# Part of an output projection's sums made between the HGRN and attention chains of a hybrid decoder layer

## The chip, the cores and the metric

One core of one Trainium2 chip. The metric is the device time of one launch in microseconds (us), the median of several runs. Kernel and reference work in float32.

## The reference

One layer with d = 1024 features and 1024 tokens. What bears on this change is its first third:

```python
x = rmsnorm(h) @ w_in                      # columns for three groups of heads
y = concat(hgrn2_mix(...),                 # 4 heads, 512 columns
           dilated_window_mix(...),        # attention, 4 heads, 256 columns
           rwkv7_mix(...))                 # 4 heads, 256 columns
h = h + y @ w_out                          # the output projection
h = h + conv_glu_ffn(rmsnorm(h), ...)      # d_ff = 2816
h = h + sigmoid(rmsnorm(h) @ w_g) * (p @ w_p)
```

## The kernel before

Activations are held transposed, as 8 row blocks of 128 features by 1024 tokens; a "half" is 512 of the tokens, and a "row half" (m, hf) is row block m of the result for half hf. Weights come as one block `[128, 1024]` (512 KB) per row block of the result: 8 tiles of 128x128, one for each row block k of the input.

**One product.** float32 is split into two fp32r parts, hi and lo, and a product is three matmuls (`mm3`, L132 to L141): hi by hi, lo of the data by hi of the weights, hi of the data by lo of the weights. A row half over all 8 k is thus 24 matmuls of 128x512. Weights are loaded by `load_w` (L102, one DMA on SP's queue into `wraw`, two buffers) and split by `split2` (L110): ScalarE (ACT) casts `whi` at L114, and VectorE (DVE) or GpSimd (POOL), by turns, subtracts `wlo` at L116. Data are split by `split_x` (cast `xh` on ACT at L160, `xl` on DVE or POOL at L162).

**Stages.** `phase_mix` (L321) normalises x and projects it; runs the RWKV heads in two passes (`rwkv`, L461), into which projections are filled as `project_rest` (L392; `FILL`, L494, says how often, and the list `js` in `rwkv` says which); then runs, with each other, four HGRN heads (`hgrn_head`, L836: chain A makes heads 0 and 2, chain B heads 1 and 3), attention (`swa`, L992, chain C) and the projections that are left (`project_late`, L429, chain F, one half of a projection, 24 matmuls into PSUM tile `zp`, per turn). The order of their turns is the string that L338 to L341 build. An input projection's result goes to DRAM as `z` and comes back as `zl` when its head begins (`zload`, L453). When a group of heads is done, its output is split into `O[k]` (`o_split`, L1100): k = 6, 7 are RWKV, k = 0 to 3 the HGRN heads, k = 4, 5 attention. `O` lies in the buffers of the projections' input, so it begins after the last turn of `project_late`.

**Output projection.** `phase_out` (L1107) loads x into `h[k]` by 8 DMAs on ACT's queue (L1114), and for each turn of the list `turns` runs `rows`: the matmuls into a PSUM tile `dp` (pool `dps`, two buffers), the weights of the turn after next, and for each half the addition to `h` on DVE (L1131) and a store of `h` for later (L1132). The turns are row 0 and row 1 with both halves, rows 2 to 7 with half 0, rows 2 to 7 with half 1. The k come in the order 6, 7, 0, 1, 4, 2, 3, 5, so that what is ready first is used first. The sum of squares of half 0 follows row by row, its reciprocal root after row 7, and `ps_ss` (L196) spreads that to all partitions.

**Behind it** comes the FFN. `ffn_first` (L1234) loads the first blocks of its weights (`raw`, L1210, SP's queue) and DVE makes sums of them (L1307, L1309, L1310), which the FFN's products need only later. A scheduler puts the instructions of each engine in order; each engine then runs its own list in order, and a DMA is issued in its turn of the list of the queue that it is on.

Of the kernel before, what the change touches and what calls it, by code (L numbers as in the profile page):

```python
# [10 lines left out]
F32 = mybir.dt.float32  # L11
# [3 lines left out]
ALU = mybir.AluOpType  # L15
# [3 lines left out]
P = 128  # L19
T = 1024  # L20
HT = 512
ND = 8
# [43 lines left out]
def interleave(order, streams):  # L66

    live = dict(streams)
    while live:
        for s in order:  # L70
            if s in live and next(live[s], STOP) is STOP:
                del live[s]


def handover(a, b, steps=14):

    for _ in range(steps):
        next(a)
        yield
    for i, _ in enumerate(b):  # L80
        if i == 1:
            for _ in a:
                yield
        yield
# [5 lines left out]
class Trunk:  # L90
# [230 lines left out]
    def phase_mix(self):  # L321
        nc, tc = self.nc, self.tc
        self.mix_norm()
        with tc.tile_pool(name="slots", bufs=1) as slots:
            self.slots, self.NSLOT = slots, 8
            self.rwkv()
        self.O, self.done = None, []
        for p in (0, 1):
            self.o_split(6 + p)
        with tc.tile_pool(name="hg", bufs=1) as slots, tc.tile_pool(name="sw", bufs=1) as sp:  # L330
            self.slots, self.NSLOT = slots, 11
            self.hgrn_setup()
            self.sp = sp
            self.swmask = sp.tile([P, T], F32, name="swmask")
            nc.scalar.dma_start(self.swmask, self.a["swm"])
            A = handover(self.hgrn_head(0), self.hgrn_head(2))
            B = handover(self.hgrn_head(1), self.hgrn_head(3))
            order = ["C", "A"] + ["M"] * 24  # L338
            for r in range(36):
                order += "C" * (r in self.TURNS) + "A" + "B" * (r > 5) + "F" * (r % 2 and r < 16)  # L340
            interleave(order, {"A": A, "B": B, "C": self.swa(sp), "F": self.project_late(self.rest), "M": self.more})  # L341

    TURNS = [i * 33 // 22 for i in range(1, 23)]

# [84 lines left out]
    def project_late(self, js):  # L429
# [20 lines left out]
        for k in self.done:  # L450
            self.o_split(k)

    def zload(self, j, pool_slot, eng=None):  # L453
        t = pool_slot("zl")
        (eng or self.nc.sync).dma_start(t, self.z[j])
        return t
# [12 lines left out]
    def rwkv(self):  # L469
        nc, tc = self.nc, self.tc  # L470
        lt = self.mix_in(0, 6, "lora")
        nc.scalar.activation(lt[0:64, :], lt[0:64, :], AF.Tanh)
        sg = self.mix_in(1, 7, "sg")
        nc.scalar.activation(sg, sg, AF.Sigmoid)
        self.z = {}
        js = iter((*range(8, 16), 24, 25, 26, 16, 17, 20, 21, 19, 23, 27, 28, 29, 18, 22))
        for p in (0, 1):
            d = {}
            with tc.tile_pool(name=f"pre{p}", bufs=1) as tp:
                self.rwkv_prep(p, tp, lt, d)  # L480
                self.rwkv_inverse(p, tp, d)
            lead, n = self.FILL[p]
            fill = self.project_rest([next(js) for _ in range(n)])
            for _ in range(8 * lead):
                next(fill)
            with tc.tile_pool(name=f"rk{p}", bufs=1) as rp:
                self.rwkv_main(p, rp, sg, d, fill)
            self.rwkv_norm(p, sg, d, 1, fill, 6 - 3 * p)
            if p == 0:
                for _ in fill:  # L490
                    pass
        self.rest, self.more = list(js), fill

    FILL = (5, 10), (4, 9)  # L494

    def rwkv_prep(self, p, tp, lt, d):

# [609 lines left out]
    def phase_out(self, hp, x0, emb):  # L1107


        nc = self.nc  # L1110
        self.h = [hp.tile([P, T], F32, name=f"h{k}") for k in range(ND)]
        self.hd = [[self.zpool.tile([P, HT], F32, tag=f"hd{k}_{hf}", name=f"hd{k}_{hf}") for hf in (0, 1)] for k in range(ND)]
        for k in range(ND):
            nc.scalar.dma_start(self.h[k], self.a["xT"][k])  # L1114
        acc = hp.tile([P, HT], F32, name="acc")

        turns = [(0, (0, 1)), (1, (0, 1)), *((m, (0,)) for m in range(2, ND)), *((m, (1,)) for m in range(2, ND))]
        ws = [self.load_w(self.a["w_out"][m]) for m, _ in turns[:2]]

        def rows(m, halves):  # L1120
            ps = self.dps.tile([P, T], F32, tag="dp", name=self.nm("dp"))
            self.dense([ps[:, :HT], ps[:, HT:]], ws.pop(0), self.O, (6, 7, 0, 1, 4, 2, 3, 5), halves)
            turns.pop(0)
            order = ExitStack()
            if len(turns) > 1:
                ws.append(self.load_w(self.a["w_out"][turns[1][0]]))
                order.enter_context(self.tc.issue_after(self.cast))
            with order:
                for g in halves:
                    u = self.h[m][:, g * HT:(g + 1) * HT]  # L1130
                    nc.vector.tensor_tensor(u, u, ps[:, g * HT:(g + 1) * HT], ALU.add)  # L1131
                    nc.scalar.dma_start(self.hd[m][g], u)  # L1132

        for m in range(ND):
            rows(m, (0, 1) if m < 2 else (0,))
            self.sq_acc(acc, self.h[m][:, :HT], m == 0)
        rows(2, (1,))
        pb = self.rstd_bcast(acc, 1.0 / 1024, EPS, self.mxp)
        x0.close()
        self.TX = {}  # L1140
        for i, n in enumerate(("p1", "p2")):
            self.TX[n] = [[self.tile16(8 * i + 2 * k + c, F32R) for c in (0, 1)] for k in range(4)]
        self.ped = [self.zpool.tile([P, T], F32, tag=f"pe{m}", name=f"pe{m}") for m in range(ND)]
        pwp = emb.enter_context(self.pool("pw"))
        px, pw = [], []
        parts = [(px, self.pxp, "pT", 0), (pw, pwp, "ple_proj", 0), (px, self.pxp, "pT", 1), (pw, pwp, "ple_proj", 1)]
        norm = self.ffn_norm(0, pb)
        for m in range(3, ND):
            rows(m, (1,))
            for _ in range(2):  # L1150
                next(norm, None)
            if parts:
                self.pe_load(pwp, *parts.pop(0))
        for m in range(ND):
            self.sq_acc(acc, self.h[m][:, HT:], m == 0)
        pb = self.rstd_bcast(acc, 1.0 / 1024, EPS, self.mxp)
        self.ffn_first()
        for m in range(5):
            self.embed(m, pw, px, self.dps.tile([P, T], F32, tag="dp", name=self.nm("dp")))
        self.pe_in = (pw, px)  # L1160
        return pb
# [552 lines left out]
```

## Time and profile before

| | |
|---|---|
| median of 3 runs | 1476.78 us (1476.26 to 1476.89) |
| time of the profiled execution | 1476.02 us |
| its span | 1474.2 us |
| TensorE's granted clock, mean | 0.992 |
| PE busy | 1420.9 us (96%) |
| DVE / ACT / POOL busy | 1053.9 / 595.8 / 383.1 us |
| RWKV with its filler | about 120 to 436 us of the span |
| HGRN and attention with `project_late` | 437 to 625 us |
| output projection | 625 to 682 us |

Times within the span are in us from its start. "busy" of an engine is time in which it executes; the rest it waits. PE is TensorE's matmul side, and its clock is the share of full speed that the chip granted. In a timeline row the columns are start, duration, engine, line, operation, output and inputs, tile sizes, and in brackets the idle time just before it and what ended it. A row of a table by stretches gives, behind each stretch, its length and the busy us (with the instructions started) of PE, PEld, DVE, ACT and POOL, then TensorE's clock, the busy share of the DMA engines and GB/s.

### The profile page before, as it was taken

To read this page: it belongs to the slowest core of one execution; us is meant where nothing else is said; L and a number is where in the kernel's file an instruction comes from. 1 tells how busy PE (TensorE), PEld (TensorE's weight loads), DVE (VectorE), ACT (ScalarE), POOL (GpSimd) and SP (SyncE) were. 2 spreads that over 40 slices of the span, in tenths; PEclk is the share of its full clock that TensorE was granted. 3 is DMA by queue.
4 is the path that set the end of the run, shared out by engine and by line. 5 is a ranking of instruction groups with operands and counts; after the bars stand their busy time and mean duration, and the time that the engine had idled before them with its cause. 6 is when DMAs were issued, how large, how long until landed. Compare 5 with 4: busy or idle time off the path is not lost.

```text
span 1474.2 us, 23335 instructions
## 1 busy us (share of the span) xinstructions
PE 1420.9 (96%) x9198; PEld 1153.4 (78%) x9198; DVE 1053.9 (71%) x1559; ACT 595.8 (40%) x984; POOL 383.1 (26%) x280
## 2 busy tenths in 40 slices
PE   6999999999999988899999999999999999999996
PEld 4778878787787666788778888888888888888885
DVE  6486243782465688647879888888888799767775
ACT  6512211313124455425544444444434544455552
POOL 2221011210122322222044444445544000002432
PEclk9999999999999999999999999999999999999998
DMA  5124102132061121174323333332333883351352
GB/s 213 43 79 133 41 31 89 47 108 80 31 228 58 58 77 54 44 279 161 135 83 114 108 102 105 108 106 96 105 108 103 312 292 97 105 163 58 119 173 101
DMA packets 79533, 167.67 MB, mean 114 GB/s; under 512 B 19904, under 2 KB 22208, under 8 KB 79424
## 3 DMA queue, kind: packets, MB, share of 16 engines
q1 hardware_dynamic: 66032, 146.39, 29.8%
q10 hardware_dynamic: 12368, 15.99, 3.1%
q0 software_dynamic: 1024, 3.80, 0.7%
q8 instruction: 72, 1.18, 0.3%
q14 instruction: 37, 0.30, 0.1%
HBM read 119.76 MB, written 46.40 MB: 113 GB/s over the span
## 4 chain that ended last, share of the span: by engine, by line
PE 48%; issue 2%; DVE 2%; POOL 1%; DMA 0%; ACT 0%; POOLq 0%; DVEq 0%; ACTq 0%
PE bg L1201 15%; PE bv L1201 12%; PE bv L1495 7%; PE bg L1495 7%; PE bv L137 1%; PE bv L139 1%; PE bv L141 1%; PE bg L137 1%; PE bg L139 1%; PE bg L141 1%; PE dp L137 1%; PE dp L139 1%; PE dp L141 1%; POOL wlo L116 0%; DVE h L1227 0%
## 5 line engine op out<-in xcount | busy, mean ns | idle before, releaser
L137 PE MATMUL dp<-xh,whi 128*128 128x512 f32 x560 | 193.0, 405 | 10.5 <-ACT xh L377 9.9
L139 PE MATMUL dp<-xl,whi 128*128 128x512 f32 x560 | 187.2, 394 | 1.2 <-DVE xl L378 1.1
L141 PE MATMUL dp<-xh,wlo 128*128 128x512 f32 x560 | 186.5, 393 | 0.3 <-POOL wlo L116 0.3
L116 POOL TENSOR_TENSOR wlo<-wraw,whi 128x512 fp32r<-128x512 f32 x60 | 82.0, 1367 | 325.5 <-ACT whi L114 290.4
L116 POOL TENSOR_TENSOR wlo<-raw,whi 128x512 fp32r<-128x512 f32 x84 | 134.8, 1624 | 76.1 <-ACT whi L114 76.1
L114 ACT CAST whi<-wraw 128x512 fp32r<-128x512 f32 x120 | 73.0, 617 | 171.9 <-PE dp L139 131.2
L1201 PE MATMUL bg<-t,whi 128*128 128x512 f32 x352 | 133.2, 389 | 0.0
L137 PEld LDWEIGHTS dp<-xh,whi 128*128 128x128 f32 x560 | 102.1, 188 | 36.2 <-ACT xh L377 9.9
L139 PEld LDWEIGHTS dp<-xl,whi 128*128 128x128 f32 x560 | 104.7, 188 | 26.0 <-DVE xl L378 3.1
L141 PEld LDWEIGHTS dp<-xh,wlo 128*128 128x128 f32 x560 | 105.3, 188 | 23.9 <-issue 1.0
L116 POOL TENSOR_TENSOR wlo<-s,whi 128x512 fp32r<-128x512 f32 x44 | 64.2, 1459 | 171.7 <-ACT whi L114 158.0
L1495 PE MATMUL bg<-t,whi 128*128 128x512 f32 x308 | 95.2, 390 | 0.0
L1495 PE MATMUL bv<-t,whi 128*128 128x512 f32 x308 | 94.8, 389 | 0.0
L114 ACT CAST whi<-raw 128x512 fp32r<-128x512 f32 x88 | 52.6, 619 | 94.6 <-issue 48.5
L114 ACT CAST whi<-s 128x512 fp32r<-128x512 f32 x66 | 38.9, 620 | 120.7 <-PE bg L1201 113.3
L1201 PEld LDWEIGHTS bg<-t,whi 128*128 128x128 f32 x352 | 66.0, 188 | 13.7
L190 POOL TENSOR_TENSOR rst<-rst,mhalf 128x4 f32<-128x4 f32 (+1 forms) x9 | 11.3, 1258 | 229.7 <-DVE rst L186 214.5
L116 DVE TENSOR_TENSOR wlo<-wraw,whi 128x512 fp32r<-128x512 f32 x60 | 47.4, 791 | 28.9 <-ACT whi L114 24.2
L1201 PE MATMUL bg<-t,wlo 128*128 128x512 f32 x176 | 67.2, 389 | 0.0
L1495 PEld LDWEIGHTS bv<-t,whi 128*128 128x128 f32 x308 | 57.8, 188 | 12.0
L1495 PEld LDWEIGHTS bg<-t,whi 128*128 128x128 f32 x308 | 57.8, 188 | 11.9
L1491 ACT CAST t<-t 128x512 fp32r<-128x512 f32 x77 | 47.8, 622 | 45.3 <-PE bv L1495 33.3
(407 smaller groups left out, 3437.4 us busy)
## 6 DMA issues: line engine op xcount, KB each, us to landing
raw<-in_ffn_up_dram SPq DMA_DIRECT2D x44, 512.0 KB, 3.6
wraw<-in_w_in_dram SPq DMA_DIRECT2D x30, 512.0 KB, 3.6
z<-zst SPq DMA_DIRECT2D x19, 512.0 KB, 3.4
gb<-ct SPq DMA_DIRECT2D x33, 256.0 KB, 2.0
t<-gb SPq DMA_DIRECT2D x33, 256.0 KB, 2.8
t<-gt SPq DMA_DIRECT2D x33, 256.0 KB, 2.7
zl<-z SPq DMA_DIRECT2D x16, 512.0 KB, 3.7
wraw<-in_ple_gate_dram SPq DMA_DIRECT2D x16, 512.0 KB, 3.7
```

The costliest lines, as they stand in the source:

```text
L114: self.cast = nc.scalar.copy(hi, src).ins
L116: eng.tensor_tensor(lo, src, hi.bitcast(F32), ALU.subtract)
L137: nc.tensor.matmul(ps[hf], wh, xh[hf], start=first, stop=False)
L139: nc.tensor.matmul(ps[hf], wh, xl[hf], start=False, stop=False)
L141: nc.tensor.matmul(ps[hf], wl, xh[hf], start=False, stop=last)
L190: nc.gpsimd.tensor_tensor(r2, r, self.mhalf[:, :n], ALU.pow)
L1201: nc.tensor.matmul(ps, w[part == 2][:, s], X[k][part == 1], start=start and k == part == 0, stop=k == 3 and part == 2, skip_group_check=no ...
L1491: nc.scalar.copy(xh, x)
L1495: nc.tensor.matmul(ps[m], wt[part == 2][:, m * P:(m + 1) * P], (xh, xl)[part == 1], start=k == part == 0, stop=k == NK - 1 and part == 2)
```

## The change

Line numbers of the code after the change are those of before plus 4 (from L343), plus 30 (from L483 on) and plus 44 (from `rows` on).

- A new chain G, `out_early`, gets ten turns (`PRE`) late in the interleaving of HGRN and attention. Each makes half of the sums of one row half of the output projection, over k = 6, 7, 0, 1: 12 matmuls into a PSUM tile `op`, one addition to a half of x that was loaded into `xe`, and a store of the result to DRAM (`hx`). The ten are (0,0), (0,1), (1,0), (1,1) and (2,0) to (7,0). Weights come as four DMAs of 128x256 for each pair of rows.
- In `phase_out` `h` is loaded by 16 half DMAs on ACT's queue, all of half 0 first, from `hx` where it exists and from x where not. Row halves that are in `hx` get the other four k only (4, 2, 3, 5) and a half load of weights (256 KB) with one split; (2,1) to (7,1) stay as they were.
- `project_late` has its turns at other places (`LATE`: 1, 3, 6, 9, 12, 15, 18, 20, 21 instead of each odd turn under 16), and one projection more (number 23, a gate of HGRN head 3): RWKV's first pass fills in at 9 instead of 10 places (`FILL`), and 23 has gone to the end of `js`.

```diff
             for r in range(36):
-                order += "C" * (r in self.TURNS) + "A" + "B" * (r > 5) + "F" * (r % 2 and r < 16)
-            interleave(order, {"A": A, "B": B, "C": self.swa(sp), "F": self.project_late(self.rest), "M": self.more})
+                order += "C" * (r in self.TURNS) + "A" + "B" * (r > 5) + "F" * (r in self.LATE) + "G" * (r in self.PRE)
+            interleave(order, {"A": A, "B": B, "C": self.swa(sp), "F": self.project_late(self.rest), "M": self.more, "G": self.out_early()})
+    LATE = (1, 3, 6, 9, 12, 15, 18, 20, 21)
+    PRE = (22, 23, 25, 26, 27, 29, 30, 31, 33, 34)
...
+    def out_early(self):
+        nc, self.hx = self.nc, {}
+        for m in range(0, ND, 2):
+            raw = self.wpool.tile([P, 1024], F32, tag="wraw", name=self.nm("wraw"), bufs=2)
+            for b in (0, 1):
+                for i, k in enumerate((6, 0)):
+                    c = (2 * b + i) * 256
+                    nc.sync.dma_start(raw[:, c:c + 256], self.a["w_out"][m + b][:, k * P:(k + 2) * P])
+            w = self.split_w(raw)
+            jobs = [[(m + b, hf) for hf in (0, 1)] for b in (0, 1)] if m == 0 else [[(m, 0), (m + 1, 0)]]
+            for job in jobs:
+                t = self.keep.tile([P, T], F32, tag="oc", name=self.nm("xe"), bufs=2)
+                half = [t[:, i * HT:(i + 1) * HT] for i in (0, 1)]
+                for u, (n, hf) in zip(half, job):
+                    nc.sync.dma_start(u, self.a["xT"][n][:, hf * HT:(hf + 1) * HT])
+                for u, (n, hf) in zip(half, job):
+                    ps = self.mxp.tile([P, HT], F32, tag="mx", name=self.nm("op"))
+                    for i, k in enumerate((6, 7, 0, 1)):
+                        self.mm3({hf: ps}, w(4 * (n % 2) + i), self.O[k], i == 0, i == 3, (hf,))
+                    nc.vector.tensor_tensor(u, u, ps, ALU.add)
+                    d = self.hx[n, hf] = self.zpool.tile([P, HT], F32, tag=f"hx{n}{hf}", name=f"hx{n}{hf}")
+                    nc.sync.dma_start(d, u)
+                    yield
...
-        js = iter((*range(8, 16), 24, 25, 26, 16, 17, 20, 21, 19, 23, 27, 28, 29, 18, 22))
+        js = iter((*range(8, 16), 24, 25, 26, 16, 17, 20, 21, 19, 27, 28, 29, 18, 22, 23))
...
-    FILL = (5, 10), (4, 9)
+    FILL = (5, 9), (4, 9)
...
-        for k in range(ND):
-            nc.scalar.dma_start(self.h[k], self.a["xT"][k])
+        for hf in (0, 1):
+            for k in range(ND):
+                nc.scalar.dma_start(self.h[k][:, hf * HT:(hf + 1) * HT],
+                                    self.hx.get((k, hf), self.a["xT"][k][:, hf * HT:(hf + 1) * HT]))
...
-        ws = [self.load_w(self.a["w_out"][m]) for m, _ in turns[:2]]
+        late = (4, 2, 3, 5)
+        def load(m, halves):
+            if (m, halves[-1]) not in self.hx:
+                return self.load_w(self.a["w_out"][m]), (6, 7, 0, 1, *late)
+            raw = self.wpool.tile([P, 1024], F32, tag="wraw", name=self.nm("wraw"), bufs=2)
+            nc.sync.dma_start(raw[:, :HT], self.a["w_out"][m][:, 2 * P:6 * P])
+            self.uid += 1
+            part = self.split2(raw[:, :HT], nc.gpsimd if self.uid % 2 else nc.vector)
+            return lambda k: [t[:, (k - 2) * P:(k - 1) * P] for t in part], late
+        ws = [load(*t) for t in turns[:2]]
 
         def rows(m, halves):
             ps = self.dps.tile([P, T], F32, tag="dp", name=self.nm("dp"))
-            self.dense([ps[:, :HT], ps[:, HT:]], ws.pop(0), self.O, (6, 7, 0, 1, 4, 2, 3, 5), halves)
+            w, ks = ws.pop(0)
+            self.dense([ps[:, :HT], ps[:, HT:]], w, self.O, ks, halves)
             turns.pop(0)
             order = ExitStack()
             if len(turns) > 1:
-                ws.append(self.load_w(self.a["w_out"][turns[1][0]]))
+                ws.append(load(*turns[1]))
                 order.enter_context(self.tc.issue_after(self.cast))
```

What this makes of the engines' lists shows at three places. The first is PE's list in the middle of the HGRN and attention stage, of before: `hsc` are scores of HGRN chunks, `swq` and `swo` products of attention, and `vt` is what HGRN heads transpose.

```order
L897 MATMUL hsc_5329<-qt_4899,ks_5269 64x64 x8
L871 MATMUL hsc_5353<-zl_5227,hk_5273 64x64 x16
L1046 MATMUL swq_5415<-zl_4765,zl_4763 128x512
L925 MATMUL vt_5375<-cst,zl_5348 128x128 x4
L925 MATMUL vt_5381<-cst,zl_5348 128x128 x4
```

The same place of the change; the three rows of `op` shown are the first of twelve alike.

```order
L927 MATMUL hsc_5334<-qt_4767,ks_5226 64x64 x8
L1076 MATMUL swq_5468<-zl_4634,zl_4632 128x256
L901 MATMUL hsc_5358<-zl_5155,hk_5230 64x64 x16
L137 MATMUL op_5395<-xh_5275,whi_5384 128x512
L139 MATMUL op_5395<-xl_5276,whi_5384 128x512
L141 MATMUL op_5395<-xh_5275,wlo_5386 128x512
```

Twelve matmuls of the output projection now stand between the scores of one HGRN head and the transposes of the next. In all, `zp` has 192 matmuls in this stage instead of 144, `op` has 108 before the last `vt` and 12 behind it, and of `dp` 18 stand before the last `vt` instead of 32.

The second place is DVE's list where the output projection begins, of before: `zl` is the last HGRN head's output, `xl` its low part, `h` the sum and `s` the FFN weights' sum from its first two loads `raw`.

```order
L986 SCALAR_TENSOR_TENSOR zl_5861<-vt_5871,par,zl_5861 128x512
L986 SCALAR_TENSOR_TENSOR zl_5861<-vt_5877,par,zl_5861 128x512
L162 TENSOR_TENSOR xl_4878<-zl_5861,xh_4877 128x512
L1131 TENSOR_TENSOR h_5906<-h_5906,dp_5959 128x512 x2
L1307 TENSOR_TENSOR s_1183_7074<-raw_6665,raw_6667 128x512
L1309 TENSOR_TENSOR s_1184_7076<-s_1183_7074,raw_6667 128x512
L1310 TENSOR_TENSOR raw_6667<-raw_6667 128x512
L1131 TENSOR_TENSOR h_5907<-h_5907,dp_6023 128x512 x2
```

The same place of the change (`h_6138` is row 0, `h_6139` row 1):

```order
L162 TENSOR_TENSOR xl_5270<-zl_6045,xh_5269 128x512
L478 TENSOR_TENSOR xe_6068<-xe_6068,op_6103 128x512
L116 TENSOR_TENSOR wlo_6306<-wraw_6302,whi_6304 128x512
L116 TENSOR_TENSOR wlo_6330<-wraw_6326,whi_6328 128x512
L1351 TENSOR_TENSOR s_1203_7162<-raw_6753,raw_6755 128x512
L1175 TENSOR_TENSOR h_6138<-h_6138,dp_6191 128x512
L1175 TENSOR_TENSOR h_6139<-h_6139,dp_6227 128x512
L1353 TENSOR_TENSOR s_1204_7164<-s_1203_7162,raw_6755 128x512
L1354 TENSOR_TENSOR raw_6755<-raw_6755 128x512
L1175 TENSOR_TENSOR h_6138<-h_6138,dp_6191 128x512
L1175 TENSOR_TENSOR h_6139<-h_6139,dp_6227 128x512
```

The additions of rows 0 and 1, of which row 0's two stood ahead of the FFN's sum, now stand behind it, first half 0 of both rows, then half 1 of both.

The third place is SP's list there, of before: `zl` is the last input of HGRN, `wraw` are weights of the output projection.

```order
L455 DMA zl_5861<-z_3834 128x1024
L1210 DMA raw_6665<-in_ffn_up_dram 128x1024
L1210 DMA raw_6667<-in_ffn_up_dram 128x1024
L1210 DMA raw_6669<-in_ffn_up_dram 128x1024
L1210 DMA raw_6671<-in_ffn_up_dram 128x1024
L105 DMA wraw_6154<-in_w_out_dram 128x1024
```

The same place of the change (`hx_6117` is the store of the last `op`):

```order
L485 DMA zl_6045<-z_5058 128x1024
L480 DMA hx_6085<-xe_6068 128x512
L1156 DMA wraw_6326<-in_w_out_dram 128x512
L1254 DMA raw_6753<-in_ffn_up_dram 128x1024
L480 DMA hx_6117<-xe_6068 128x512
L1156 DMA wraw_6350<-in_w_out_dram 128x512
L1254 DMA raw_6755<-in_ffn_up_dram 128x1024
L105 DMA wraw_6374<-in_w_out_dram 128x1024
L1254 DMA raw_6757<-in_ffn_up_dram 128x1024
```

The second FFN load, which the FFN's first sum needs, now stands behind the store of the last `op` and behind a load of weights.

## The prediction

> **What bounds the kernel now.** I read the page's sums first, then the clock by slices, then the two stages that the change touches by stretches, then the waits.
>
> ```profile
> PE 1420.9 (96%) x9198; PEld 1153.4 (78%) x9198; DVE 1053.9 (71%) x1559; ACT 595.8 (40%) x984; POOL 383.1 (26%) x280
> ...
> PEclk9999999999999999999999999999999999999998
> ```
>
> PE is busy for 1420.9 of 1474.2 us. Matmuls that only move from one stage to another therefore gain nothing by themselves: PE's work stays what it is. The change can gain only where PE now waits or runs at a lower clock, and that must be inside the stage that receives the matmuls. So I measured that stage, in busy us of PE, PEld, DVE, ACT and POOL, with the clock behind:
>
> ```profile
> 436.70:508.70 72.00, 71.43 (x579) 53.65 (x578) 40.13 (x91) 34.11 (x76) 15.08 (x13) 1.00 0.22 78
> 508.70:540.00 31.30, 24.20 (x289) 19.52 (x288) 25.90 (x44) 14.36 (x33) 11.23 (x11) 0.89 0.23 76
> 540.00:570.00 30.00, 26.47 (x255) 18.34 (x254) 24.29 (x51) 16.43 (x40) 10.62 (x8) 0.94 0.21 72
> 570.00:600.00 30.00, 26.22 (x272) 19.56 (x274) 24.35 (x57) 18.06 (x36) 4.73 (x4) 1.00 0.11 36
> 600.00:625.00 25.00, 23.20 (x233) 20.19 (x230) 14.50 (x28) 9.23 (x18) 5.55 (x5) 1.00 0.13 43
> sum 188.30, PE 171.53 PEld 131.25 DVE 129.17 ACT 92.19 POOL 47.22; mean PE 34.30 PEld 26.25 DVE 25.83 ACT 18.44 POOL 9.44
> ```
>
> PE works 171.5 of 188.3 us: it idles 16.8 us, nearly all after 508.7, where DVE is busy for as long as PE or longer. There the HGRN and attention chains go hand over hand and PE has run out of projections. The stage loses a second thing, the clock:
>
> ```profile
> 512.00:518.50 6.50, 1.73 (x15) 1.17 (x11) 6.50 (x10) 1.20 (x3) 3.63 (x4) 1.00 0.50 162
> 518.50:525.40 6.90, 6.66 (x51) 5.28 (x51) 3.57 (x9) 3.31 (x9) 0.00 (x0) 0.51 0.32 116
> ...
> 557.60:566.00 8.40, 6.06 (x78) 5.07 (x76) 8.07 (x11) 3.30 (x7) 3.60 (x4) 0.80 0.05 17
> ```
>
> After 6.5 us in which PE worked 1.7, the next 6.9 us ran at 0.51: 3.4 us lost. The stretch from 557.6 lost 8.4 x 0.2 = 1.7 us in the same way. **So 16.8 + 5.0, about 21.8 us, is all that the change can win.**
>
> **The change part by part.** First the size of what moves, from the output projection's pace:
>
> ```profile
> 629.02 0.62 PE L137 MATMUL dp<-xh,whi 128*128 128x512 f32 x2
> ...
> 634.95 0.62 PE L139 MATMUL dp<-xl,whi 128*128 128x512 f32 x2
> ```
>
> These are rows of two matmuls; from the first to the last lie 13 rows, so one matmul takes 5.93 / 26 = 0.228 us. Ten row halves of 12 take 27.3 us out of the output projection, and the projection 23 takes 48 x 0.228 = 10.9 us out of RWKV. The receiving stage gets 38.2 us of matmuls for 21.8 us of holes, so it lengthens, and what counts is how many holes stay.
>
> *RWKV gives 10.9 us away.* That it gets shorter by just that needs its filler to have been in the way and not in a hole:
>
> ```profile
> 120.00:270.00 150.00, 150.00 (x1614) 121.08 (x1614) 56.06 (x111) 37.46 (x60) 19.54 (x14) 1.00 0.22 68
> ```
>
> PE has no idle time in the first pass, and the one place of ten that goes is a small part of its filler. I take the transfer at nothing; if the pass ran out of cover somewhere, up to the same 10.9 us would turn into waits, but PE waits for nothing between 120 and 270 now.
>
> *Holes that stay in the stage.* I go by the four places where PE has little of its own and DVE much:
>
> ```profile
> 489.20:503.00 13.80, 13.71 (x133) 10.69 (x132) 9.52 (x21) 6.02 (x13) 0.00 (x0) 1.00 0.19 58
> 508.70:521.20 12.50, 7.49 (x63) 5.04 (x63) 10.93 (x16) 4.60 (x10) 6.93 (x6) 0.89 0.40 134
> 533.20:548.00 14.80, 12.46 (x130) 9.92 (x126) 14.73 (x35) 9.83 (x25) 4.77 (x5) 1.00 0.11 37
> 617.17 0.39 PE L967 MATMUL hpo<-hst,qt 128*128 128x128 f32 x2
> 623.93 1.06 PE L985 MATMUL vt<-cst,ho 128*128 128x128 f32 x8 [1.80 <-DVE ho L979]
> ```
>
> (a) In 489 to 521 DVE has 20.5 us of work to PE's 21.2, in bursts: 2.5 us left. (b) In 533 to 566 DVE is the busier engine (14.7 of 14.8 us, 8.1 of 8.4). Two blocks of 24 and one of 12 go in, 13.7 us against holes of 4.7 us and the clock: 2 us left. (c) From the last `hpo` to `vt` runs a chain through DVE, POOL and DVE of 623.93 - 617.17 - 0.39 = 6.4 us; beside it stand 12 matmuls of `op` and 12 of `dp` now, 5.5 us: 1 us left. (d) 1.5 us elsewhere. Together **7.0 us stay, and the clock is kept: -14.8 us**. The bounds: 0 us left (-21.8), and 14 left if DVE sets the pace (below).
>
> *Small things in the stage.* Ten additions on DVE and four further table loads on ACT:
>
> ```profile
> L1131 DVE TENSOR_TENSOR h<-h,dp x16: 672/686/689, 630.6 to 708.1; 128x512 f32<-128x512 f32 x16
> 264.54 1.28 ACT L531 ACT_TABLE_LOAD   x1
> ```
>
> 6.9 us on DVE (plus 5 or so of weight splits and a gate's product) come on 129 of some 206 us, 5.1 us on ACT on 92; both are inside (a) to (d). The loads of x and stores of `hx` (some 5 MB) go over DMA engines that move 36 to 78 GB/s in the stretches above. Nothing for them.
>
> *The output projection's start, where a new wait arises.* In before these rows show it (DVE, then the DMA issues):
>
> ```profile
> 630.61 1.28 DVE L1131 TENSOR_TENSOR h<-h,dp 128x512 f32<-128x512 f32 x2 [2.69 <-PE dp L141]
> 635.61 0.69 DVE L1307 TENSOR_TENSOR s<-raw,raw 128x512 f32<-128x512 f32 x1 [3.71 <-DMA raw<-in_ffn_up_dram]
> 636.34 0.69 DVE L1309 TENSOR_TENSOR s<-s,raw 128x512 f32<-128x512 f32 x1
> 636.95 0.69 DVE L1310 TENSOR_TENSOR raw<-raw 128x512 f32<-128x512 f32 x1
> 640.14 1.28 DVE L1131 TENSOR_TENSOR h<-h,dp 128x512 f32<-128x512 f32 x2 [2.51 <-PE dp L141]
> ...
> DMA to landing us min/median/max: 7.4/9.6/12.7
> ```
>
> The FFN sum at L1307 stood idle for 3.7 us until the second FFN load landed, at 635.6, 7.4 us after its issue (the last row: loads of `raw` around 626 to 642). That cost nothing: row 0's additions were ahead of it, so row 0's PSUM tile was free for row 2 by 632, and PE had rows 1 and 2 to do. In the change, row 0's and row 1's additions are **behind** that sum on DVE, and only two `dp` tiles exist: row 2 can't begin until row 0's second half has been added.
>
> Count from PE's last `vt` (625.0 in before) as t = 0. PE then has 12 matmuls of `op` and 30 of rows 0 and 1, 42 x 0.228 = 9.6 us, where before it had 64 of `dp`. The second FFN load waits on its queue for the last `hx` store: `op` ends at about 2.8, but DVE first does 1.41 (L986), ACT's cast and 1.23 (L162), so the addition is done at about 4.0, and after the store and row 7's weights the load is issued at about 4.7 (before: 3.0). With 7.4 us of landing it is there at 12, in DMA traffic like this:
>
> ```profile
> 625.00:635.00 10.00, 9.93 (x43) 7.61 (x43) 3.52 (x5) 1.24 (x2) 1.30 (x1) 1.00 0.79 292
> 635.00:645.00 10.00, 10.00 (x46) 8.29 (x45) 3.87 (x6) 3.32 (x6) 2.53 (x2) 1.00 1.02 394
> L1114 ACTq DMA_DIRECT2D h<-in_xT_dram x8: 334/382/862, 626.0 to 635.4; - x8
> ...
> DMA to landing us min/median/max: 3.5/9.2/12.0
> ```
>
> The sum, two additions, two more sums and the next addition are six operations of 0.69 us: row 0 is out at 12 + 4.1 = 16. The second half of row 0's `h` is the ninth load on ACT's queue; issued a little after the eight of before (whose issues end 10 us from the start, at 9.2 us each to land) it gives about 17 at worst. PE has work until 9.6: **a wait of 6 to 8 us, taken as 7.0**. Its bounds are 0 (the load at 3.6 us, the median over all its 44 on the page's last part, is there by 8.3, which leaves under 3) and 16 (below).
>
> After such a gap comes the clock: the row 512.00:518.50 above has 4.8 us of gaps and is followed by 3.4 us lost. A gap of 7 should cost one such loss or a part: 2.5 us. The Trainium skill, "TensorE: Matmul & The Clock Gate", Part 1 on the HAM clock gate, says that after an idle window of about 3.4 us the array runs at half clock until it has been busy for as long. By that rule the loss is one window at half speed, an estimate of 1.7 us, or two with an unlucky phase; the trace's 6.9 us at 0.51 agree with two.
>
> *Behind it* rows 2 to 7 have 12 matmuls (2.7 us) each and a 256 KB load each, half of both, at the same ratio; PE stays the longer one. No term.
>
> **The sum**: -14.8 + 7.0 + 2.5 = -5.3, so 1476.02 - 5.3 = 1470.7 on the profiled execution. The median of the runs lies 0.76 above that execution: **1471.5 us**.
>
> **The rivals.** In medians:
>
> *A longer wait at row 2 (slower).* One mechanism: loads of `h` and `raw` crowd the DMA queues while PE's work ahead of the wait has shrunk from 64 to 42 matmuls. If row 0's second half of `h` is issued at about 13 and lands in the slowest 12.0 us of the row above, row 0 is out at 25.6, a wait of 16 and 3.4 of clock: -14.8 + 19.4 = +4.6, 1481.4. It decides from where wait and clock reach 14.8, a wait of about 11.4. For it: DMA at 1.02 in 635 to 645. Against: FFN loads took 7.4 to 12.7 there, and half loads are smaller. 0.17.
>
> *No wait.* The second FFN load lands quickly, since the `h` loads before it are half as large, and DVE is through by t = 10. -14.8: 1462.0. For it: 3.6 us as the page's median of such loads. Against: 292 GB/s in that stretch. 0.20. The Trainium skill, same page, "Architectural detail", has ScalarE and VectorE take their queues strictly in order; by that the additions cannot pass the sum, which speaks against this case, and L1307's 3.71 us with nothing done meanwhile agrees.
>
> *VectorE sets the pace of the mixing stage.* It is busy 129 us there, and from 508.7 to 600 for 74.5 of 91.3 us, to which 12 us come. If the matmuls put between the steps only delay the chain that DVE goes through, 14 us of holes stay: -7.8 + 9.5 = +1.7, 1478.5. For it: 14.73 of 14.80. Against: a projection block there is longer than any DVE step, and the waits of PE are few:
>
> ```profile
> PE swt L1069 <- ACT ob L1083: 4.2, 2, 3.9
> PE vt L985 <- DVE ho L979: 4.1, 3, 1.8
> PE swd L204 <- DVE hS L875: 2.1, 1, 2.1
> ```
>
> 0.18. That the change doesn't do what it says is out: the order shows `op` between the chains.
>
> **How the numbers follow.** The forecast has 0.45. About 0.2% (2.95 us) is what a measurement here can tell from no change. The forecast's own range is 1466 to 1476 (wait from 3 to 11). Faster by more: most of the forecast (0.38) and no wait (0.20), 0.58. Within: 0.07 of the forecast, 0.08 of VectorE's case, 0.03 of the long wait: 0.18. Slower: 0.14 of the long wait and 0.10 of VectorE's: 0.24. The range takes in no wait at its good end and the long wait: 1460.5 to 1481.5.
>
> **What would show it.** The stage up to the last `vt` should grow from 188.3 by 17.5 us (48 + 108 - 14 = 142 matmuls, 32.3 us, less 14.8), which with RWKV's 10.9 less puts `vt`'s end at about 631.6. PE's idle time in it should be near 7 us and the clock 1.00. At the output projection's start, DVE's FFN sum should wait some 6 us for `raw`, PE's first matmul of row 2 some 7 us, and the clock should dip behind. No wait of row 2 refutes that step; holes of 12 us or more ahead of `vt` refute the first. A wait in RWKV's first pass of over 2 us would be a cost that I left out.

## The result, and the profile after

The kernel with the change takes 1482.1 us (median of 5, 1480.2 to 1485.1), the kernel before 1476.5 us (5 runs): **slower by 0.4%, ratio 1.0040 (95% interval 1.0025 to 1.0055)**. Forecast were 1471.5 us and a faster kernel; 1482.1 lies just above the range, which ended at 1481.5. The profiled span is 1480.8 us, 6.6 more than before.

PE's strip (busy tenths in 40 slices of the span) of the kernel before:

```profile
PE   6999999999999988899999999999999999999996
```

The page's sums and the two strips that changed, kernel after:

```profile
PE 1426.0 (96%) x9198; PEld 1155.8 (78%) x9198; DVE 1062.0 (72%) x1574; ACT 601.2 (41%) x989; POOL 381.3 (26%) x277
...
PE   6999999999999999969999999999999999999996
...
PEclk9999999999999999989999999999999999999998
```

The three digits of 8 of before lie in the stage of HGRN and attention (slices of 37 us); they are 9 now, and a 6 has come in the slice around 650 us, where the output projection starts. Two waits of PE in the kernel after (what it waited for, us in all, times, longest):

```profile
PE dp L137 <- DVE h L1175: 10.6, 1, 10.6
...
PE ps_ss L196 <- POOL rst L190: 5.3, 4, 2.6
```

and by stretches, kernel after (the stage of HGRN and attention begins at 423.6; its last `vt` ends at 637.56):

```profile
423.60:440.00 16.40, 15.59 (x126) 12.27 (x125) 8.46 (x20) 7.53 (x18) 6.87 (x6) 1.00 0.40 129
440.00:470.00 30.00, 29.72 (x277) 20.75 (x276) 18.31 (x43) 16.56 (x41) 4.64 (x5) 1.00 0.11 37
...
530.00:550.00 20.00, 19.14 (x99) 13.05 (x98) 14.55 (x23) 11.57 (x20) 6.76 (x5) 0.83 0.29 92
550.00:570.00 20.00, 18.88 (x166) 13.68 (x166) 16.40 (x32) 15.86 (x30) 8.31 (x7) 1.00 0.29 94
...
637.30:647.20 9.90, 9.88 (x45) 7.72 (x43) 4.85 (x7) 2.49 (x4) 1.29 (x1) 1.00 0.50 163
647.20:657.80 10.60, 0.00 (x0) 0.00 (x0) 3.52 (x7) 0.00 (x0) 0.00 (x0) 0.72 1.03 394
657.80:665.00 7.20, 7.19 (x23) 5.81 (x24) 1.92 (x3) 2.32 (x4) 0.00 (x0) 0.70 0.85 321
```

For 10.6 us PE does nothing at all while the DMA engines are fully busy (share 1.03, 394 GB/s), and then it runs 7.2 us at 0.70.

To compare kernels I cut each trace at the same four events of PE: the first transposes of attention's values (`vt` at 434.50 in before), the end of the last `vt` of HGRN, the first `ps_ss` of L196 (the reciprocal root behind half 0 of the output projection), and the FFN's first product (`bv`). A stage contains different numbers of 128x512 matmuls of `zp`, `op` and `dp` in different kernels, so I also give what is left of the stage when each of them is taken off at 0.2275 us: the HGRN and attention chains' own work, with holes and slow clock. For the phase behind I take all its matmuls off in the same way; eight small ones of `ps_ss` are among them, the same eight in every kernel. Each row is one traced execution. The rows from the third on are the kernels of the experiments below. In us:

| kernel | stage begins | last `vt` ends | `ps_ss` | FFN | stage: length, matmuls, **left** | output phase: length, matmuls, **left** |
|---|---|---|---|---|---|---|
| before | 434.5 | 625.0 | 681.5 | 724.6 | 190.5, 177, **150.2** | 56.5, 245, **0.8** |
| after | 423.6 | 637.6 | 687.2 | 731.5 | 214.0, 319, **141.4** | 49.7, 153, **14.9** |
| rows first | 423.3 | 637.7 | 683.0 | 728.9 | 214.5, 319, **141.9** | 45.3, 152, **10.7** |
| FFN's sums behind | 424.1 | 638.1 | 686.4 | 729.0 | 214.0, 319, **141.4** | 48.3, 153, **13.5** |
| all three edits | 423.7 | 637.9 | 684.4 | 730.2 | 214.2, 319, **141.6** | 46.5, 151, **12.2** |
| halves late | 424.0 | 637.8 | 679.1 | 725.2 | 213.8, 319, **141.2** | 41.4, 154, **6.3** |
| FFN loads late too | 424.0 | 637.3 | 678.0 | 724.0 | 213.3, 319, **140.8** | 40.7, 154, **5.6** |
| sums only | 434.2 | 649.6 | 698.7 | 745.0 | 215.4, 270, **154.0** | 49.1, 151, **14.7** |
| **projections only** | 423.8 | 617.1 | 672.4 | 717.3 | 193.3, 227, **141.7** | 55.3, 242, **0.3** |
| four sums | 422.9 | 625.1 | 685.4 | 729.8 | 202.3, 253, **144.7** | 60.2, 217, **10.9** |
| spread only | 433.8 | 622.8 | 680.7 | 725.2 | 189.0, 177, **148.7** | 57.9, 245, **2.2** |
| one more, early | 423.6 | 630.9 | 687.9 | 731.2 | 207.3, 225, **156.1** | 57.0, 244, **1.5** |
| two more | 416.8 | 619.9 | 676.3 | 719.4 | 203.1, 273, **141.0** | 56.5, 245, **0.7** |
| last one sooner | 423.0 | 616.6 | 672.0 | 716.9 | 193.7, 227, **142.0** | 55.4, 242, **0.3** |

The two bold columns tell the story: the change wins 8.8 us in the stage and loses 14.1 in the phase behind. One row needs care: the traced execution of "projections only" is the slowest of its four (1468.6 us at a mean clock of 0.991; the others took 1464.4 to 1465.5 at 0.994), so this row is some 3 us long for that kernel; in which stage, no trace shows. From `bv` to PE's last matmul all kernels agree within 1.5 us (741.3 to 742.8).

### The profile page after: what moved, and what is told of

It reads as the page before. It is cut to its first block, busy times and chain, and to the rows that moved or that the text cites. A ratio compares the mean times of both kernels' runs of the same rounds, so it can differ in the third digit from the quotient of the medians.

```text
span 1480.8 us, 23404 instructions
## 1 busy us (share of the span) xinstructions
PE 1426.0 (96%) x9198; PEld 1155.8 (78%) x9198; DVE 1062.0 (72%) x1574; ACT 601.2 (41%) x989; POOL 381.3 (26%) x277
## 4 chain that ended last, share of the span: by engine, by line
PE 48%; issue 2%; POOL 1%; DVE 1%; DMA 1%; ACT 0%; POOLq 0%; ACTq 0%; DVEq 0%
PE bg L1245 15%; PE bv L1245 12%; PE bv L1539 7%; PE bg L1539 7%; PE bv L137 1%; PE bv L139 1%; PE bv L141 1%; PE dp L141 1%; PE dp L137 1%; PE dp L139 1%; PE bg L137 1%; PE bg L139 1%; PE bg L141 1%; DMA pe<-pst 0%; POOL wlo L116 0%
## 5 line engine op out<-in xcount | busy, mean ns | idle before, releaser
L137 PE MATMUL dp<-xh,whi 128*128 128x512 f32 x504 | 174.7, 408 | 20.4 <-DVE h L1175 10.6
L139 PE MATMUL dp<-xl,whi 128*128 128x512 f32 x504 | 168.1, 395 | 0.8 <-DVE xl L382 0.8
L141 PE MATMUL dp<-xh,wlo 128*128 128x512 f32 x504 | 167.9, 394 | 0.3 <-POOL wlo L116 0.3
L137 PEld LDWEIGHTS dp<-xh,whi 128*128 128x128 f32 x504 | 92.2, 190 | 44.1 <-DVE h L1175 11.0
L139 PEld LDWEIGHTS dp<-xl,whi 128*128 128x128 f32 x504 | 94.9, 189 | 23.2 <-DVE xl L382 2.5
L141 PEld LDWEIGHTS dp<-xh,wlo 128*128 128x128 f32 x504 | 95.5, 189 | 22.1 <-issue 1.0
L116 DVE TENSOR_TENSOR wlo<-wraw,whi 128x512 fp32r<-128x512 f32 x63 | 50.8, 806 | 32.5 <-ACT whi L114 25.6
L190 POOL TENSOR_TENSOR rst<-rst,mhalf 128x4 f32<-128x4 f32 (+1 forms) x9 | 11.3, 1259 | 230.4 <-DVE rst L186 214.5
L1539 PEld LDWEIGHTS bg<-t,whi 128*128 128x128 f32 x308 | 57.7, 188 | 11.9
```

What stands on the lines that cost most here:

```text
L116: eng.tensor_tensor(lo, src, hi.bitcast(F32), ALU.subtract)
L137: nc.tensor.matmul(ps[hf], wh, xh[hf], start=first, stop=False)
L139: nc.tensor.matmul(ps[hf], wh, xl[hf], start=False, stop=False)
L141: nc.tensor.matmul(ps[hf], wl, xh[hf], start=False, stop=last)
L190: nc.gpsimd.tensor_tensor(r2, r, self.mhalf[:, :n], ALU.pow)
L1539: nc.tensor.matmul(ps[m], wt[part == 2][:, m * P:(m + 1) * P], (xh, xl)[part == 1], start=k == part == 0, stop=k == NK - 1 and part == 2)
```

## The experiments

**Rows 0 and 1 of h first.** Only the order of the 16 half loads of `h`.

```diff
-        for hf in (0, 1):
-            for k in range(ND):
+        firsts = [(0, 0), (0, 1), (1, 0), (1, 1)]
+        for k, hf in firsts + [(k, hf) for hf in (0, 1) for k in range(2, ND)]:
```

> Only the order of the 16 half loads of h changes: rows 0 and 1 with both halves come first. Theory H (row 2's wait of 10.6 us is set by the landing of row 0's second half of h, the ninth on ACT's queue, at 657.0): that half is now second, lands at about 649, row 2 waits 3 to 4 us, the clock dips less, and the time falls from 1482.1 by 7 to 9 us, to 1473 to 1475. Theory S, that of the prediction (VectorE's FFN sum ahead of the additions sets the wait): nothing moves ahead of that sum, so 1480 to 1484.

**The FFN's first sums behind rows 0 and 1.** Only their place on VectorE; `add1` is the last addition of row 1.

```diff
-            sums(d)
+            with self.tc.issue_after(self.add1):
+                sums(d)
```

> Only the place of the FFN's first sums on VectorE changes: behind the additions of rows 0 and 1. Theory H: row 0's second half still lands at 657, so the wait stays at 10 to 11 us and the time at 1480 to 1484. Theory S: the additions are free to run when the sums of the rows are there, the wait falls below 3 us and the time to 1472 to 1475.

Measured: 1480.5 us for the first (10 runs, 1476.1 to 1482.3; ratio 1.0028, 1.0018 to 1.0038), 1482.7 for the second (4 runs; 1.0044, 1.0028 to 1.0060). VectorE in the kernel after shows why the second changes nothing:

```profile
646.74 0.69 DVE L1351 TENSOR_TENSOR s<-raw,raw 128x512 f32<-128x512 f32 x1 [2.71 <-DMA raw<-in_ffn_up_dram]
647.40 0.69 DVE L1175 TENSOR_TENSOR h<-h,dp 128x512 f32<-128x512 f32 x1
649.05 0.69 DVE L1175 TENSOR_TENSOR h<-h,dp 128x512 f32<-128x512 f32 x1 [0.96 <-DMA h<-hx]
649.66 0.68 DVE L1353 TENSOR_TENSOR s<-s,raw 128x512 f32<-128x512 f32 x1
650.26 0.68 DVE L1354 TENSOR_TENSOR raw<-raw 128x512 f32<-128x512 f32 x1
657.06 1.36 DVE L1175 TENSOR_TENSOR h<-h,dp 128x512 f32<-128x512 f32 x2 [6.12 <-DMA h<-hx]
```

The FFN's sum is done at 647.4, when PE has only just run out of work. What is missing until 657.06 is row 0's second half of `h`. In the second experiment PE's wait there is 10.6 us again. In the first it is short:

```profile
649.61 0.50 PE L137 MATMUL dp<-xh,whi 128*128 128x512 f32 x1 [2.27 <-DVE h L1177]
653.33 0.50 PE L137 MATMUL dp<-xh,whi 128*128 128x512 f32 x1 [0.70 <-DVE h L1177]
667.05 0.50 PE L137 MATMUL dp<-xh,whi 128*128 128x512 f32 x1 [2.55 <-ACT whi L114]
668.08 0.50 PE L141 MATMUL dp<-xh,wlo 128*128 128x512 f32 x1 [0.29 <-DVE wlo L116]
683.01 1.11 PE L196 MATMUL ps_ss<-cst,rst 128*128 128x128 f32 x4 [4.40 <-POOL rst L190]
```

So theory H holds for the wait, and S, which was my prediction's, falls, though the time of the first lies in S's range. Theory H's time was wrong: 10.6 us of wait became 3.0, and only 4.2 us arrive at `ps_ss`, since two others came, for weights (2.6) and for the sum of squares (4.4 instead of 2.6).

**Three edits together.** Rows first, FFN's sums behind, and the weight casts of rows 5 and 6 behind the first four loads of `h` on ACT.

```diff
+                with ExitStack() as ahead:
+                    if m in (3, 4) and halves == (0,):
+                        ahead.enter_context(self.tc.issue_after(self.hfirst))
+                    ws.append(load(*turns[1]))
```

> Three edits together: rows 0 and 1 of h first, the weight casts of rows 5 and 6 behind those four loads on ACT (so that the loads begin 4 us earlier), and the FFN's sums behind the additions. Theory H: row 2 waits under 1.5 us and the clock keeps at 1.00, so 12 to 13 us are won: 1469 to 1471, below the 1476.5 of before. Theory S: no better than the kernel that moves only the FFN's sums, and over 1472.

Measured: 1482.4 us (4 runs; 1.0043, 1.0026 to 1.0059). PE does not wait at row 2 at all, and nothing is won. The wait has moved, PE's timeline:

```profile
659.27 0.69 PE L137 MATMUL dp<-xh,whi 128*128 128x512 f32 x1 [3.65 <-ACT whi L114]
668.36 0.47 PE L137 MATMUL dp<-xh,whi 128*128 128x512 f32 x1 [1.64 <-DVE h L1180]
684.40 1.11 PE L196 MATMUL ps_ss<-cst,rst 128*128 128x128 f32 x4 [5.04 <-POOL rst L190]
```

Theory H was right about row 2 and wrong about the time; S had the time (no better than the second experiment) and was wrong about row 2. The loads of `h` do begin 1.3 us behind the last `vt` here, instead of 5.6. But the cast that PE waits 3.65 us for stands on ACT behind a step that itself waits 16.54 us for loads of `h`, and the next load of weights is issued only at 660.18.

**The second halves of h late.** Rows first, and rows 2 to 7 get their second half only behind their first half's store.

```diff
-        for k, hf in firsts + [(k, hf) for hf in (0, 1) for k in range(2, ND)]:
+        for k, hf in firsts + [(k, 0) for k in range(2, ND)]:
...
+                if m > 1 and halves == (0,):
+                    nc.scalar.dma_start(self.h[m][:, HT:], self.a["xT"][m][:, HT:])
```

> As the kernel with rows 0 and 1 of h first, and the second halves of h for rows 2 to 7 are loaded only behind the first half's store. Theory O (the wait of row 2 went, but the same bytes then kept the weights of row half (2,1) and the sum of squares late): the weights' wait of 2.6 us goes and the reciprocal root's wait falls from 4.4 to under 3: 1475 to 1478. Theory D (the DMA engines have more to move in this phase than fits beside PE's shorter work, so a wait only changes its place): 1479 to 1482.

**The FFN's first loads late too**, behind the last weights of the output projection:

```diff
-            d["raw"], d["rav"] = self.load_up(d["f"]), self.load_up(NFF + d["f"])
+            with self.tc.issue_after(self.wdma):
+                d["raw"], d["rav"] = self.load_up(d["f"]), self.load_up(NFF + d["f"])
```

> The change with rows 0 and 1 of h first, second halves of h late, and now also the FFN's four first loads (2 MB) behind the last weights of the output projection. Theory D (after the early sums the phase is short of DMA time, 400 GB/s at a share of 1.0 from 647 to 665): 2 MB less are 5 us of it, the waits of row 2 and of the weights fall below 1 us in all, 1470 to 1473. Rival Q (what is left are waits of queues and of ACT's and DVE's order): 1475 to 1477.

Measured: 1476.3 us (10 runs; 1.0004, 0.9994 to 1.0013) and 1474.8 us (10 runs; 0.9988, 0.9979 to 0.9998); the two intervals just overlap. The first is theory O's number, but only half its mechanism: the reciprocal root's wait falls to 0.6 us, while the weights' wait of 2.6 us stays. Stretches of it, from the last `vt` on:

```profile
637.80:647.50 9.70, 9.57 (x42) 7.43 (x40) 4.54 (x7) 2.49 (x4) 1.29 (x1) 1.00 0.49 176
647.50:655.00 7.50, 4.80 (x20) 3.61 (x21) 4.63 (x8) 0.21 (x1) 0.00 (x0) 1.00 1.03 401
655.00:665.00 10.00, 9.89 (x44) 7.87 (x42) 4.52 (x8) 5.08 (x9) 0.00 (x0) 1.00 0.98 365
```

and of the second:

```profile
647.50:655.00 7.50, 5.84 (x26) 4.48 (x25) 2.18 (x4) 1.26 (x2) 0.00 (x0) 1.00 0.99 341
655.00:665.00 10.00, 8.37 (x37) 6.58 (x36) 5.71 (x9) 4.54 (x8) 1.40 (x1) 1.00 0.80 281
```

2 MB less take the DMA share from 0.98 to 0.80 in 655 to 665 and win only 0.7 us of what is left of the phase (6.3 to 5.6). Theory D's time is missed, and Q's is the nearer one. Of these 5.6 us the trace shows 1.7 at row 2 and 2.6 at the weights of (2,1):

```profile
664.16 1.76 DVE L116 TENSOR_TENSOR wlo<-wraw,whi 128x512 fp32r<-128x512 f32 x1
665.97 0.50 PE L141 MATMUL dp<-xh,wlo 128*128 128x512 f32 x1 [2.60 <-DVE wlo L116]
```

The 2.6 us are the same in both kernels, though the DMA share of the stretch up to 665 is 0.98 in the one and 0.80 in the other. In both, VectorE makes these weights' low part right behind a row's addition and its sum of squares; that is an order of a list, as Q says. The 1.7 us at row 2 end with a load of `h`, in a stretch whose DMA share is still 0.99, so there theory D isn't refuted. The Trainium skill, "DMA: Bandwidth & Descriptors", section "Where 436 GB/s comes from", gives 435 GB/s as the ceiling of a core's ports and about 358 GB/s as the limit of the HBM side. The 394 to 401 GB/s that the traces show at a share of 1.03 lie above the second and within a tenth of the first.

**Sums only.** Projection 23 back in RWKV, the late projections at the early turns of before.

```diff
-    LATE = (1, 3, 6, 9, 12, 15, 18, 20, 21)
+    LATE = (1, 3, 5, 7, 9, 11, 13, 15)
-        js = iter((*range(8, 16), 24, 25, 26, 16, 17, 20, 21, 19, 27, 28, 29, 18, 22, 23))
+        js = iter((*range(8, 16), 24, 25, 26, 16, 17, 20, 21, 19, 23, 27, 28, 29, 18, 22))
-    FILL = (5, 9), (4, 9)
+    FILL = (5, 10), (4, 9)
```

> The early sums of ten row halves alone: projection 23 is back in RWKV, and the late projections have the early turns of before (1, 3, 5 to 15). Theory M (the wider projections filled the hole of before at 512 to 525, the sums the later ones): that hole and its half clock come back, some 5 to 7 us, less 2 for fewer blocks: 1485 to 1487. Rival: the ten sums alone fill what can be filled and 23 only moves work: 1480 to 1483.

**Projections only.** No early sums; `hx` is empty, so the output projection computes all of its sums as before.

```diff
-        for m in range(0, ND, 2):
+        for m in range(0):
```

> No early sums: only the wider projections (nine turns, number 23 from RWKV), the output projection computes everything itself as before, though h still comes as half loads. Theory M (what the HGRN and attention stage won, it won by the projections; the early sums only move work and load the output projection's start): the stage wins back 6 to 10 of its holes, the output projection stays as before: 1467 to 1472. Rival (only the two together fill the stage): 1475 to 1480.

Measured: 1494.0 us for the sums alone (4 runs; 1.0122, 1.0101 to 1.0144), and **1465.2 us for the projections alone** (4 runs, 1464.4 to 1468.6; 0.9921, 0.9904 to 0.9938). Theory M had the sign of both and was too mild in both: it gave the sums alone 1485 to 1487 and the projections alone 1467 to 1472. Against the projections alone, the ten sums of the change thus cost some 17 us. The stages of the four kernels, each by its own events (before, after, sums only, projections only):

```profile
434.50:624.99 190.49, 173.72 (x1634) 132.96 (x1633) 131.20 (x271) 94.16 (x201) 47.78 (x40) 0.97 0.19 65
```

```profile
423.58:637.56 213.98, 207.50 (x1776) 159.11 (x1775) 144.40 (x290) 106.18 (x216) 53.59 (x44) 0.98 0.29 93
```

```profile
434.23:649.62 215.39, 197.92 (x1727) 151.52 (x1726) 143.60 (x282) 98.64 (x209) 56.09 (x45) 0.96 0.25 88
```

```profile
423.75:617.06 193.31, 185.78 (x1684) 143.40 (x1683) 131.95 (x275) 101.84 (x209) 49.29 (x42) 0.97 0.22 78
```

PE's idle time (length less PE's busy time) is 16.8, 6.5, 17.5 and 7.5 us. The projections alone close the holes; the sums alone leave them open and only make the stage longer; and on top of the projections the sums close one microsecond more. What is left of the stage says the same: 150.2 before, 141.7 with the projections, 141.4 with both.

Where the sums stand says much of why. The first `op` begins at 561.07 in the kernel after, 137.5 us behind the start of the stage. The stages of before, after and projections only, each cut at that place:

```profile
434.50:572.00 137.50, 125.08 (x1144) 94.03 (x1143) 94.30 (x194) 68.82 (x154) 37.80 (x32) 0.96 0.22 74
572.00:624.99 52.99, 48.63 (x492) 38.93 (x491) 36.90 (x78) 25.34 (x48) 9.98 (x8) 1.00 0.12 41
```

```profile
423.58:561.07 137.49, 134.33 (x1180) 100.88 (x1178) 95.69 (x200) 74.75 (x158) 38.89 (x33) 0.98 0.28 89
561.07:637.56 76.49, 73.16 (x601) 58.24 (x598) 48.70 (x91) 31.43 (x59) 14.69 (x11) 1.00 0.30 101
```

```profile
423.75:561.07 137.32, 134.95 (x1190) 102.05 (x1189) 95.62 (x201) 75.22 (x159) 38.57 (x34) 0.98 0.23 82
561.07:617.06 55.99, 50.84 (x496) 41.35 (x495) 36.33 (x75) 26.63 (x51) 10.72 (x9) 0.97 0.19 66
```

Of the 16.8 us of holes of before, 12.4 lie ahead of that place, where no sum stands, and 4.4 behind it. There the projections alone leave 5.2 us, and the sums bring them to 3.3.

**Four sums.** Early sums for rows 0 and 1 only, with the projections of the change and rows first.

```diff
-        for m in range(0, ND, 2):
+        for m in (0,):
-    PRE = (22, 23, 25, 26, 27, 29, 30, 31, 33, 34)
+    PRE = (25, 29, 31, 34)
```

> Early sums for rows 0 and 1 alone (four halves, turns 25, 29, 31, 34), rows 0 and 1 of h first, wider projections as in the change. Theory M with a small share of sums: 48 matmuls find holes worth 2 to 4 us and the output projection keeps 72 matmuls more as cover than with ten: 1468 to 1473. Rival (each early sum costs the stage as much as it takes from the phase behind): as the kernel without early sums or slower, over 1474.

Measured: 1480.9 us (10 runs; 1.0030, 1.0021 to 1.0040): the rival holds. The stage wins nothing by them (144.7 left, 141.7 without any sum), and row 2 waits again, for a load of `h`. I put that down to three FFN loads, which SP issues from 631.25 on, just ahead of the loads of `h` from 632.41 on; no run separates it:

```profile
641.76 0.79 PE L137 MATMUL dp<-xh,whi 128*128 128x512 f32 x1 [6.83 <-DVE h L1177]
```

**Which part of the projections.** All without early sums: the wider turns alone with 23 in RWKV; 23 late, but at close turns; two projections late (28 too); and the last block one turn sooner. Of each edit only the new lines are shown:

```diff
+    LATE = (1, 3, 6, 9, 12, 15, 18)                      # spread only; js and FILL of before
+    LATE = (1, 3, 5, 7, 9, 11, 13, 15, 17)               # one more, early
+    LATE = (1, 2, 4, 6, 9, 12, 15, 18, 20, 22, 24)       # two more
+    FILL = (5, 8), (4, 9)                                # two more
+    LATE = (1, 3, 6, 9, 12, 15, 18, 19, 21)              # last one sooner
```

> No early sums, projection 23 in RWKV as before; only the wider turns of the late projections (1, 3, 6, 9, 12, 15, 18). Theory W (the gain of the kernel without early sums is from where the blocks stand): most of its 11 us stays: 1466 to 1470. Rival N (it is from the further projection, whose two blocks fill the holes at 526 to 549): 1473 to 1477.

> No early sums; the further projection (23), but the late projections at each odd turn from 1 to 17, close together as before. Theory N (the further projection brings the gain, since its two blocks reach stretches that had none): the blocks end earlier than 549, the holes behind stay, yet most of the gain stays: 1466 to 1470. Rival B (spread and number are needed together: blocks this early push work that was not waiting, and the holes at 512 to 566 of before remain): 1474 to 1478.

> No early sums, and a second projection (28) moved from RWKV's first pass to the late ones, whose turns are 1, 2, 4, 6, 9, 12, 15, 18, 20, 22, 24. If what is left of holes in the stage (7.5 us of idle time in the kernel without early sums) can be filled by two more blocks, it takes 2 to 5 us off that kernel: 1460 to 1463. If RWKV's first pass runs out of cover, or the blocks only push VectorE's chain: 1465 to 1472.

> The kernel without early sums, its last projection block one turn earlier (19 instead of 20). Theory C (TensorE's clock drops to a half at 540 to 546 since the 7.5 us ahead hold only small matmuls, though PE idles for under 1 us there): the block comes into that stretch, the dip of 3 us goes: 1461 to 1464. Rival: the dip comes later, behind the next such stretch: 1465 to 1468.

Measured: spread only 1475.8 us (10 runs; 0.9998, 0.9989 to 1.0008); one more, early 1480.8 us (9 runs; 1.0033, 1.0021 to 1.0044); two more 1469.8 us (4 runs; 0.9953, 0.9938 to 0.9968); last one sooner 1468.8 us (4 runs; 0.9959, 0.9944 to 0.9974).

Neither half of the edit does it. Spreading alone leaves 15.9 us of idle time in the stage (its length less PE's busy time), the further projection at early turns 17.7; both together leave 7.5. First N was right against W, then B against N, though 1480.8 us lies above B's range too: blocks must be there *and* stand where PE would wait. Two more came out in the second of its two ranges (1465 to 1472). The stage then starts only 7.0 us earlier than with one (416.8 against 423.8), though 10.9 us of matmuls left RWKV: a wait of RWKV's own chain, which the other kernels don't list, has come.

```profile
PE yt L738 <- DVE y L731: 2.6, 1, 2.6
```

With the last block one turn sooner, the clock's dip only moved (rows of 15 us: projections only, then last one sooner; the clock is the first number behind the last bracket):

```profile
535.00:550.00 15.00, 14.14 (x76) 9.48 (x75) 12.75 (x22) 8.89 (x16) 3.94 (x4) 0.77 0.16 54
550.00:565.00 15.00, 14.17 (x164) 10.44 (x163) 13.51 (x26) 13.97 (x28) 7.93 (x7) 1.00 0.16 55
```

```profile
535.00:550.00 15.00, 11.07 (x76) 7.83 (x76) 14.81 (x21) 11.09 (x17) 8.28 (x5) 0.95 0.15 54
550.00:565.00 15.00, 14.86 (x151) 10.15 (x150) 12.32 (x21) 10.65 (x24) 6.04 (x5) 0.82 0.15 54
```

15 x 0.23 = 3.4 us lost in the one, 0.8 + 2.7 in the other. But the second dip isn't of the same kind: it comes behind a wait of PE of 3.93 us.

```profile
548.08 0.55 PE L1099 MATMUL swt<-cst,lg 128*128 128x128 f32 x3 [3.93 <-DVE hS L929]
```

So theory C falls and the rival holds in that the dip only moves; the median lies 0.8 us above its range. The first two rows are of the slowest execution of that kernel, and the other three had a higher mean clock (0.994), so in those the clock dipped less, there or elsewhere. The best kernel of the study stays the one with the projections only.

## Why the prediction was wrong, point by point

- *RWKV gives 10.9 us away at no cost.* Right: the stage starts at 423.58 instead of 434.50.
- *Holes that stay: -14.8.* **Failed first.** The idle time was nearly as said (6.5 us for 7.0), but what is left of the stage fell by 8.8, not 14.8. Of the six, 3.4 come from "the clock is kept": 20 us at 0.83. A block costs more than its matmuls: the nine `op` blocks ahead of `vt` fill 26.3 us of PE's list where 108 x 0.2275 are 24.6; that is 1.7. Some 1.4 us I can't place. What failed more deeply is what I took to fill the holes. I counted 38 us of matmuls against 22 of holes as one heap; the traces show that 8.5 of the 8.8 come from the two blocks of projection 23 together with the wider turns, and 0.3 from the ten sums, which begin behind 12.4 of the 16.8 us of holes. Two readings were off as well. VectorE is "busy for as long as PE or longer" only in the first of the four rows behind 508.7, and "489 to 521" leaves out the 5.7 us between its two rows.
- *The wait at row 2: 7.0 us.* It is 10.6, at the place forecast, by another cause. The FFN load that I made the cause landed early (the sum waited 2.71, not 6), and moving the sum changes nothing. The load of `h` that I gave "about 17 at worst" decides: VectorE takes it at 657.06, 19.5 us behind the end of the last `vt`. The prediction's own terms, an issue behind 10 us and 9.2 us to land, add up to 19 and not to 17, so a wait near 10 us stood in my own rows. I had its queue begin about where that of before did, 1.0 us behind that `vt`; it begins 5.6 us behind, since ACT casts the weights of row 6 first, and that cast waits for PE. The eighth and the ninth load are issued from 650.72 on:

```profile
642.69 0.62 ACT L114 CAST whi<-wraw 128x512 fp32r<-128x512 f32 x1 [1.93 <-PE dp L139]
643.12 4.62 ACTq L1145 DMA_DIRECT2D h<-hx  x6
650.72 0.93 ACTq L1145 DMA_DIRECT2D h<-hx  x2
```

  The rival of the longer wait had this mechanism and the right sign. It had the issue right, at about 13 us behind the `vt`; but the load then took about 6 us and not 12.0. That its time, 1481.4, comes close to the 1482.1 measured is luck: its wait and clock are some 6 us too long, and its stage is 6.0 too short.
- *Clock behind it: 2.5 us.* 7.2 us at 0.70 are 2.2. Right.
- *Rows 2 to 7: "No term."* Failed. The reciprocal root's wait at `ps_ss` is 2.6 us instead of 1.0, which the kernel before shows:

```profile
681.50 0.65 PE L196 MATMUL ps_ss<-cst,rst 128*128 128x128 f32 x4 [1.03 <-POOL rst L190]
```

  Once the first wait is removed, weights and sums of squares take its place: 10.7 us are left of the phase with rows first, 5.6 in the best version. I read it so: a row's matmuls, and with them the cover (the work that PE has while loads land), were halved, but not its loads and stores of `h`.
- *Behind that* 1.6 us from `ps_ss` of the second half to the FFN (12.1 against 10.5). PE's clock is 0.70 from 719.4 to 725.0 there. It isn't the change's: kernels of this study have either 10.5 or 11.9 to 12.6 there whatever their edits (before, FFN's sums behind, two more: 10.5; projections only, rows first: 12.1).
- *The sum.* -5.3 forecast, +6.6 of span measured: 6.0 from the stage, 3.6 from row 2, 1.6 from the reciprocal root and 1.6 from the clock ahead of the FFN, less 0.3 for the clock behind row 2, come to 12.5, where 11.9 lie between the two.

VectorE's rival didn't come out as put: the idle time fell to 6.5, not 14. What stays open: some 1.4 us of the stage, why the 3.3 us of holes behind 561.07 stay beside the sums, and what holds the 1.7 us at row 2 in the best version.

## What to carry to other kernels

Filler closes a hole only at the place where the engine waits; count it hole by hole, in the order of the engine's list, and let a run with each part alone say which part pays. Work that is taken out of a phase takes that phase's cover with it: its loads, stores and casts stay, and here the ninth load of a queue became the bound. Removing one such wait by reordering only pays if the loads and casts behind it have cover too.

## What the runs showed of the hardware

TensorE's clock dropped with PE idle for less than 1 us. In the kernel after, PE worked 4.14 of the 5 us from 535, on small matmuls, with one gap of 0.86, and the next 5 us were granted 0.50:

```profile
535.00:540.00 5.00, 4.14 (x24) 1.73 (x24) 5.00 (x11) 4.94 (x8) 0.00 (x0) 0.92 0.00 0
540.00:545.00 5.00, 5.00 (x27) 3.98 (x26) 4.66 (x9) 2.08 (x5) 2.28 (x2) 0.50 0.14 54
```

The Trainium skill, "TensorE: Matmul & The Clock Gate", Part 1, puts the drop to half clock behind an idle window of about 3.4 us; here no gap is longer than 0.86 us, so a shorter gap can be enough. That stretch holds only matmuls that are 64 wide on one side; whether it is the gap or their size that does it, no run here separates. In the kernel with the last block one turn sooner the dip stands behind a wait of 3.93 us, as the page has it.
